# Forming dt of the state space part early, and eleven rotating tiles instead of four for its masked decays, in a hybrid two-layer backbone

## The chip, the cores and the metric

The kernel runs on one core of a Trainium2 chip. The metric is the device time of one execution in microseconds (us); the median of three runs before the change is 1880.62 us (1880.29 to 1880.88). The engines of the core work side by side, each through its own instructions in a fixed order: TensorE (PE in the profile; PEld is its loading of weights), VectorE (DVE), ScalarE (ACT), GpSimd (Pool, written POOL in rows) and SyncE (SP, which issues most DMAs).

## The reference, cut to what matters

Two trunk layers act on 256 context and 256 latent tokens of width 1024. Each layer is a gated feed-forward part, a token mixer and a second feed-forward part. The mixer projects the tokens, splits the width into three groups of heads (a gated linear recurrence, a neighbourhood attention, and a state space part with 8 heads in both directions) and projects the three back. The state space part, in one direction:

```python
    z, xs, bm, cm, dtf, dtb = mamba2_prepare(lat[8], lat[9], lat[10], lat[11], conv_w, conv_b, dt_bias)
    # dtf = softplus(dt_f + dt_bias[0]); xs, bm, cm = silu(conv(...)) split in three
    cum = jnp.cumsum(dtr * A.reshape(G, R), axis=2)
    seg = cum[:, :, :, None] - cum[:, :, None, :]
    Lm = jnp.where(causal[None, None, :, :, None, None], jnp.exp(jnp.minimum(seg, 0.0)), 0.0)
    cb = jnp.einsum('bctgn,bcsgn->bctsg', Cr, Br)
    y_diag = jnp.einsum('bctsg,bctsgr,bcsgr,bcsgrp->bctgrp', cb, Lm, dtr, xr)
    decay_end = jnp.exp(jnp.minimum(cum[:, :, -1:] - cum, 0.0))
    states = jnp.einsum('bcsgn,bcsgr,bcsgrp->bcgrpn', Br, decay_end * dtr, xr)
...
    return rms_norm(y * jax.nn.silu(z), w)
```

The last line is the gate by `z` that closes the state space part.

## The kernel before

All activations stay on the chip; weights stream in from memory. Each large product is made of three products of split halves (lines 675, 676 and 677), here called dense products. They make up most of what PE does. What lies between them, the mixer's small products, is called short here.

The mixer of a layer is written as a table, MIX_ORDER: `feat`, `feats` and `tok` make projections of columns, `go` starts one of the three head groups (`hg` the recurrence, `na` the attention, `ssm` the state space part) as a generator, and `run` advances the started groups. The table gives the program's order. A scheduler then places the instructions of each engine by their priority, which follows the program's order, and by what each waits for; dense products fill the gaps of the groups. Tiles come from rings: a tag of the table TAGS has so many buffers, and a new tile of a tag waits until the tile that had its buffer is no longer read.

The function `dt` has two halves. Lines 1258 to 1280 form dt (its columns come with those of the attention's values, the step `("tok", C_VA)`) and split the decay's exponent into `ah` and `al`. Lines 1285 to 1293 sum it up over tokens on PE, take the exponential on ACT (`ex`, L1288) and form the weights of the states on DVE (L1293).

The function `ssm` then runs in three stages. First, Pool multiplies the inputs by the skip gain (L1307), and six units of the recurrence over chunks follow: weights times inputs into `s` on DVE (L1313), the states on PE (L1317), their copy on ACT (L1321), and the product with C on PE (L1330) with DVE behind it (L1333, L1335). Second, the part inside the chunks: for every chunk of 128 tokens (four in layer 0, two in layer 1) L1342 forms C times B on PE and L1346 masks it on DVE, then for each of the two groups Pool builds four masked decays `gm` with affine_select (L1354), PE sums them (L1358), ACT takes the exponential (L1362) and scales (L1366), DVE combines (L1367, L1369), and PE multiplies with the inputs (L1374); DVE adds the result up (L1376). There are 32 masks in layer 0 and 16 in layer 1. Third, after the projection of `z`: the gate (L1382), squares (L1383), a Newton chain of small DVE operations for the root (L557 to L565), the norm (L1386) and transposes (L1391).

The gate itself, silu of `z`, is formed in `z_in` (L1400), and its tiles `zs` are taken from the ring `gm` too, four in layer 0 and two in layer 1. Next to all this run the attention's scores (L1191), softmax (L1194 to L1205), products (L1207, L1210) and final norm (L1215, a Newton chain, L1218, the transposes L1223). L873 and L874 split the results into `qk` and `mx`, which the output projection reads. L291 and L294 split the incoming weights into halves on ACT and DVE.

Silu and Exp sit in different tables of ACT. When an instruction needs the table that isn't loaded, an ACT_TABLE_LOAD stands ahead of it, under the same line.

Of the kernel before, what the change touches and what calls it, by code (L numbers as in the profile page):

```python
# [38 lines left out]
NORM_PRIO = 200  # L39
NGW = 10  # L40
TAGS = {"V": 1, "V2": 1, "ga": 1, "T": 1, "kS": 1, "gs": 2, "h2": 6, "mx": 4, "qk": 4, "n2": 4, "cv": 1, "bc": 4, "xf": 2,
        "bt": 1, "gm": 4, "ew": 2, "cb": 1, "s2": 3}
FPARTS = [range(0, NF // 2), range(NF // 2, NF)]


C_Q, C_FF, C_FB, C_I, C_G = 0, 256, 512, 768, 1024
C_QA, C_KA, C_VA = 1280, 1536, 1792
C_Z, C_XBC, C_DT = 2048, 2560, 3584
C_XS, C_B, C_C = C_XBC, C_XBC + 512, C_XBC + 768
# [108 lines left out]
def second(n):  # L158
# [13 lines left out]
MIX_ORDER = [  # L172
    [
        ("feats", C_FF, C_FB, C_Q, C_G), ("go", "hg", 0), ("feat", C_QA + 128), ("tok", C_I),
        ("feat", C_XS + 384), ("tok", C_VA), ("feat", C_B), ("feat", C_B + 128), ("feat", C_C + 128),
        ("feat", C_C), ("run", 2), ("run", 4), ("feat", C_XS), ("feat", C_XS + 128), ("feat", C_XS + 256),
        ("feat", C_KA), ("dt",), ("go", "ssm"), ("run", 999), ("feat", C_QA), ("feat", C_KA + 128),
        ("go", "na"), ("run", 999), ("feats1", C_FF + 128, C_FB + 128, C_Q + 128, C_G + 128), ("go", "hg", 1),
        ("run", 999), ("tok", C_Z), ("tok", C_Z + 256), ("run", 999),
    ],  # L180
    [
        ("feats", C_FF, C_FB, C_Q, C_G), ("go", "hg", 0), ("tok", C_I), ("run", 999), ("tok", C_VA),
        ("feat", C_B), ("feat", C_KA), ("run", 6), ("feat", C_C + 128), ("run", 999), ("feat", C_QA),
        ("feat", C_B + 128), ("feat", C_C), ("feats1", C_FF + 128, C_FB + 128, C_Q + 128, C_G + 128),
        ("go", "hg", 1), ("run", 999), ("feat", C_XS), ("feat", C_XS + 128), ("feat", C_XS + 256),
        ("feat", C_XS + 384), ("dt",), ("go", "ssm"), ("run", 999), ("feat", C_KA + 128),
        ("feat", C_QA + 128), ("go", "na"), ("run", 999), ("tok", C_Z), ("tok", C_Z + 256), ("run", 999),
    ],
]
# [1372 lines left out]
```

## Time and profile before

| | us |
|---|---|
| median of three runs | 1880.62 |
| profiled execution | 1881.97 |
| its span on the core | 1880.2 |
| PE busy | 1852.1 |
| DVE busy | 1317.0 |
| ACT busy | 724.8 |
| Pool busy | 59.3 |

The profiled execution is one more run, taken with the profiler; its span is the time from its first to its last instruction. A row of a timeline gives the start, the length, the engine, the line of the kernel, the operation, output and input, and in brackets how long the engine was idle before it and which instruction ended that. A product's row is longer than its share of PE's time, since products overlap: the starts of neighbouring rows tell the pace. The mixer of layer 0 lies between about 445 and 690 us of the span, that of layer 1 between about 1470 and 1690.

### The profile page before, as it was taken

What the parts mean: (1) busy time and instruction counts of PE and PEld (TensorE: products, weight loads), DVE (VectorE), ACT (ScalarE), POOL (GpSimd) and SP (SyncE); (2) the same over time, 40 slices, a digit from 0 to 9 for tenths busy, and PEclk for the clock granted to TensorE, in tenths of its full rate; (3) what the DMA queues carried; (4) which work ended last, traced back from release to release, by engine and by line L of the source; (5) the groups of instructions that cost most, each with busy time, mean ns of one, the idle gap of its engine ahead of it and who ended that gap; (6) DMA issues with size and microseconds to landing.
All of it is one profiled execution on the core that took longest, in us unless ns stands there. A gap on an engine that the chain in (4) does not pass through costs nothing.

```text
span 1880.2 us, 28238 instructions
## 1 busy us (share of the span) xinstructions
PE 1852.1 (99%) x11235; PEld 1596.1 (85%) x11235; DVE 1317.0 (70%) x2324; ACT 724.8 (39%) x1160; POOL 59.3 (3%) x76
## 2 busy tenths in 40 slices
PE   9999999999999999999999999999999999999998
PEld 7788888899777889888888898888889987889998
DVE  7677877875877677677733557777637668887565
ACT  4332223334425544232223342222234455465454
POOL 1000000000014000000000000000000000210000
PEclk9999999999999999999999999999999999999999
DMA  8466666634212134566533536666434422245554
GB/s 307 156 193 194 197 190 194 185 138 124 79 40 62 47 116 143 163 195 192 163 94 101 158 112 189 193 194 194 126 101 154 144 91 74 91 142 183 181 180 134
DMA packets 76964, 277.83 MB, mean 148 GB/s; under 512 B 8608, under 2 KB 10016, under 8 KB 76320
## 3 DMA queue, kind: packets, MB, share of 16 engines
q1 hardware_dynamic: 75312, 272.88, 46.2%
q10 hardware_dynamic: 1520, 3.15, 0.5%
q8 instruction: 88, 1.44, 0.3%
q14 instruction: 44, 0.36, 0.1%
HBM read 269.71 MB, written 5.24 MB: 146 GB/s over the span
## 4 chain that ended last, share of the span: by engine, by line
PE 92%; DVE 6%; ACT 1%; issue 1%; DMA 0%; SPq 0%; DVEq 0%; ACTq 0%
PE psd L675 28%; PE psd L676 27%; PE psd L677 27%; PE psm L1069 1%; DVE junk L516 1%; PE psm L1191 1%; PE psm L1207 1%; PE psm L1317 1%; PE psm L1374 1%; DVE ew L1367 1%; PE psm L1330 1%; DVE lo L294 0%; PE psm L1358 0%; PE psm L592 0%; PE psm L578 0%
## 5 line engine op out<-in xcount | busy, mean ns | idle before, releaser
L294 DVE TENSOR_TENSOR lo<-raw,hi 128x1024 fp32r<-128x1024 f32 x328 | 403.7, 1231 | 369.0 <-ACT hi L291 365.4
L291 ACT CAST hi<-raw 128x1024 fp32r<-128x1024 f32 x332 | 348.6, 1050 | 715.8 <-PE psd L676 664.5
L675 PE MATMUL psd<-h,hi 128*128 128x512 f32 (+1 forms) x1456 | 539.0, 372 | 2.0 <-ACT h L655 1.0
L676 PE MATMUL psd<-h,hi 128*128 128x512 f32 (+1 forms) x1456 | 537.7, 370 | 0.5 <-DVE h L656 0.5
L677 PE MATMUL psd<-h,lo 128*128 128x512 f32 (+1 forms) x1456 | 536.5, 370 | 0.2 <-DVE lo L294 0.2
L516 DVE CUSTOM_DVE_ANT_0 junk<-wm,csb,par 128x1024 bf16<-128x1024 f32 x256 | 327.8, 1280 | 2.4
L675 PEld LDWEIGHTS psd<-h,hi 128*128 128x128 f32 x1456 | 273.5, 189 | 50.0 <-issue 1.5
L677 PEld LDWEIGHTS psd<-h,lo 128*128 128x128 f32 x1456 | 274.1, 188 | 48.4 <-issue 1.5
L676 PEld LDWEIGHTS psd<-h,hi 128*128 128x128 f32 x1456 | 274.6, 189 | 45.6 <-DVE h L656 0.9
L675 PE MATMUL psd<-gh,hi 128*128 128x512 f32 (+1 forms) x605 | 216.8, 358 | 0.0
L677 PE MATMUL psd<-gh,lo 128*128 128x512 f32 (+1 forms) x605 | 216.4, 358 | 0.0
L676 PE MATMUL psd<-gl,hi 128*128 128x512 f32 (+1 forms) x605 | 216.4, 358 | 0.0
L675 PEld LDWEIGHTS psd<-gh,hi 128*128 128x128 f32 x605 | 114.3, 189 | 17.0 <-ACT gh L813 0.3
L676 PEld LDWEIGHTS psd<-gl,hi 128*128 128x128 f32 x605 | 114.2, 189 | 16.7
L677 PEld LDWEIGHTS psd<-gh,lo 128*128 128x128 f32 x605 | 114.2, 189 | 16.7
L676 PE MATMUL psd<-raw,hi 128*128 128x258 f32 x352 | 99.7, 284 | 0.0
L675 PE MATMUL psd<-raw,hi 128*128 128x258 f32 x352 | 99.6, 284 | 0.0
L677 PE MATMUL psd<-raw,lo 128*128 128x258 f32 x352 | 99.3, 284 | 0.0
L813 ACT CAST gh<-silu 128x512 fp32r<-128x512 f32 (+1 forms) x88 | 49.7, 566 | 86.0 <-DVE silu L810 83.6
L544 DVE SCALAR_TENSOR_TENSOR x<-psd,gate,x 128x256 f32<-128x256 f32 x112 | 52.0, 480 | 36.6 <-PE psd L677 35.8
L675 PE MATMUL psd<-hi,h 128*128 128x256 f32 (+1 forms) x224 | 65.9, 295 | 1.4 <-ACT ga L1037 1.3
L675 PEld LDWEIGHTS psd<-raw,hi 128*128 128x128 f32 x352 | 67.0, 190 | 0.0
(276 smaller groups left out, 2435.5 us busy)
## 6 DMA issues: line engine op xcount, KB each, us to landing
raw<-in_wst SPq DMA_DIRECT2D x349, 512.0 KB, 3.6
wm<-in_wmod SPq DMA_DIRECT2D x128, 512.0 KB, 4.1
ws<-in_wm SPq DMA_DIRECT2D x8, 512.0 KB, 9.9
xd<-x SPq DMA_DIRECT2D x2, 2048.0 KB, 6.5
x<-xd SPq DMA_DIRECT2D x8, 512.0 KB, 4.1
wc<-in_wmod SPq DMA_DIRECT2D x7, 512.0 KB, 10.0
x<-in_xt SPq DMA_DIRECT2D x4, 512.0 KB, 5.3
n<-in_bias SPq DMA_DIRECT2D x8, 256.0 KB, 3.3
```

Of the source, the lines that this page charges most:

```text
L291: cut = nc.scalar.copy(hi, r)
L294: ins = e.tensor_tensor(out=lo, in0=r, in1=hi.bitcast(F32), op=ALU.subtract)
L516: self.nc.vector.tensor_tensor_reduce(junk, w, self.csb[:, v], 1.0, self.p(l, "bmod", j), ALU.mult, ALU.add, accum_out=self.mod[l][:, j, v ...
L544: ins = nc.vector.scalar_tensor_tensor(out=self.x[:, d, a:b], in0=ps[:, a - off:b - off], scalar=gate[:, d, v:v + 1], in1=self.x[:, d, a:b ...
L675: mm(ps, wh, xh, start=start, stop=False)
L676: mm(ps, wh, xl, start=False, stop=False)
L677: mm(ps, wl, xh, start=False, stop=stop)
L813: nc.scalar.copy(a[:, lo:hi], s[:, lo:hi])
L1069: nc.tensor.matmul(ps[r, s], kc[r, s], q(r, c * 64), start=True, stop=True)
L1191: nc.tensor.matmul(ps[:, :nk], self.qk[h2][r, t * P:(t + 1) * P], self.qk[2 + h2][r, :nk], start=True, stop=True)
L1207: nc.tensor.matmul(ps[:, hc], pT[:, k * P:(k + 1) * P], self.V[:, k, 256 + h * 64:256 + h * 64 + 64], start=k == 0, stop=k == nk // P - 1)
L1317: nc.tensor.matmul(ps[:, g * 256:g * 256 + 256], bt[:, t, g * P:(g + 1) * P], xw[:, g * 256:g * 256 + 256], start=True, stop=True)
```

## The change

Three edits. The step `("dt",)` stands directly behind `("tok", C_VA)` in both layers, and no longer in front of `("go", "ssm")`. The ring `gm` has 11 buffers of 2 KB per partition instead of 4. The memory for them comes from the scratch space that the program keeps for DMAs with descriptors made at run time, which is set to 1024 bytes.

```diff
 TAGS = {"V": 1, "V2": 1, "ga": 1, "T": 1, "kS": 1, "gs": 2, "h2": 6, "mx": 4, "qk": 4, "n2": 4, "cv": 1, "bc": 4, "xf": 2,
-        "bt": 1, "gm": 4, "ew": 2, "cb": 1, "s2": 3}
+        "bt": 1, "gm": 11, "ew": 2, "cb": 1, "s2": 3}
...
-        ("feat", C_XS + 384), ("tok", C_VA), ("feat", C_B), ("feat", C_B + 128), ("feat", C_C + 128),
+        ("feat", C_XS + 384), ("tok", C_VA), ("dt",), ("feat", C_B), ("feat", C_B + 128), ("feat", C_C + 128),
         ("feat", C_C), ("run", 2), ("run", 4), ("feat", C_XS), ("feat", C_XS + 128), ("feat", C_XS + 256),
-        ("feat", C_KA), ("dt",), ("go", "ssm"), ("run", 999), ("feat", C_QA), ("feat", C_KA + 128),
+        ("feat", C_KA), ("go", "ssm"), ("run", 999), ("feat", C_QA), ("feat", C_KA + 128),
...
-        ("feats", C_FF, C_FB, C_Q, C_G), ("go", "hg", 0), ("tok", C_I), ("run", 999), ("tok", C_VA),
+        ("feats", C_FF, C_FB, C_Q, C_G), ("go", "hg", 0), ("tok", C_I), ("run", 999), ("tok", C_VA), ("dt",),
...
-        ("feat", C_XS + 384), ("dt",), ("go", "ssm"), ("run", 999), ("feat", C_KA + 128),
+        ("feat", C_XS + 384), ("go", "ssm"), ("run", 999), ("feat", C_KA + 128),
...
-    nc = bacc.Bacc("TRN2", target_bir_lowering=False, num_devices=1)
+    nc = bacc.Bacc("TRN2", target_bir_lowering=False, num_devices=1, dynamic_dma_scratch_size=1024)
```

The order of instructions moves at three places. The first is DVE in layer 0, ahead of the first state of the state space part. The names are those of the program, with the numbers of tiles left in; `ga`, `T` and `dec` belong to the recurrence. Before:

```order
L1094 TENSOR_TENSOR ga_3568<-ga_3568,T_3569 128x16x32 x2
L1096 TENSOR_TENSOR T_3569<-T_3569 128x2x8
L1100 COPY dec_4455<-T_3569 128x16
L1293 TENSOR_TENSOR dtk_3898<-ex_4411,dtk_3898 128x4x8 x2
L1313 TENSOR_TENSOR s_712_4442<-x,dtk_3898 128x512
```

and with the change:

```order
L1094 TENSOR_TENSOR ga_3568<-ga_3568,T_3569 128x16x32 x2
L1313 TENSOR_TENSOR s_712_4442<-x,dtk_3898 128x512
L1096 TENSOR_TENSOR T_3569<-T_3569 128x2x8
L1100 COPY dec_4455<-T_3569 128x16
L1333 TENSOR_TENSOR s_716_4452<-psm_4449,ex_3936 128x512
```

L1293 now stands some 48 rows further up, between convolutions, and L1313 comes directly behind L1094. On PE the five products of L1285 leave the place ahead of L1105 in the same way and stand some 180 rows further up.

The second is ACT at the end of layer 1's mixer. `ew` and `cb` belong to the state space part, `n` to the attention, `hi` to the weights' split, and `gm` here are the tiles `zs`. Before:

```order
L1366 ACTIVATE ew_13876<-cb_13860,dtk_12898 128x128
L1366 ACTIVATE ew_13906<-cb_13860,dtk_12898 128x128 x4
L1205 COPY n_2225_14146<-psm_14141 128x512
L1215 ACTIVATE n_2226_14153,nss_13989<-no_13990 128x256
L291 CAST hi_14437<-raw_14435 128x1024
L1362 ACTIVATE ew_13906<-psm_13893 128x512
L1400 ACT_TABLE_LOAD
L1400 ACTIVATE gm_14247<-psd_14186 128x256
L1400 ACTIVATE gm_14248<-psd_14186 128x256
L1215 ACTIVATE n_2227_14155,nss_13989<-no_13991 128x256
```

and with the change:

```order
L1400 ACT_TABLE_LOAD
L1400 ACTIVATE gm_14248<-psd_14186 128x256
L1400 ACTIVATE gm_14247<-psd_14251 128x256
L1366 ACTIVATE ew_13876<-cb_13860,dtk_12898 128x128 x2
L1362 ACT_TABLE_LOAD
L1362 ACTIVATE ew_13876<-psm_13863 128x512
L1366 ACTIVATE ew_13876<-cb_13860,dtk_12898 128x128 x2
L1366 ACTIVATE ew_13906<-cb_13860,dtk_12898 128x128 x4
L1205 COPY n_2225_14146<-psm_14141 128x512
L1215 ACTIVATE n_2226_14153,nss_13989<-no_13990 128x256
L1400 ACT_TABLE_LOAD
L1400 ACTIVATE gm_14248<-psd_14251 128x256
```

Behind the last of these rows stand another load and L1362 for `ew_13906`, and ahead of the first a load, one L1400, a load and L1362 for the unit before. So the four L1400 have moved from behind the last L1362 to places between the L1362, and where one load stood there are six.

The third is PE at the same place, from the last but one L1374 on. L1358 reads the masks, L1207 belongs to the attention, and `mx` and `qk` in a dense product name what the output projection reads. Before:

```order
L1374 MATMUL psm_13887<-x,ew_13876 128x64 x4
L1358 MATMUL psm_13893<-gm_13894,slr 128x512
...
L1207 MATMUL psm_14134<-V_12552,n_2225_14146 128x64 x4
L1374 MATMUL psm_13917<-x,ew_13906 128x64 x4
L675 MATMUL psd_14401<-mx_12776,hi_14284 128x256
...
L677 MATMUL psd_14402<-mx_13502,lo_14285 128x256
L1223 MATMUL psm_14172<-con,no_13990 128x128
L1223 MATMUL psm_14179<-con,no_13990 128x128
```

and with the change:

```order
L1374 MATMUL psm_13887<-x,ew_13876 128x64 x4
L1358 MATMUL psm_13893<-gm_13894,slr 128x512
...
L1207 MATMUL psm_14134<-V_12552,n_2225_14146 128x64 x4
L675 MATMUL psd_14402<-mx_12776,hi_14284 128x256
...
L677 MATMUL psd_14402<-mx_13535,lo_14285 128x256
L1374 MATMUL psm_13917<-x,ew_13906 128x64 x4
L1223 MATMUL psm_14172<-con,no_13990 128x128
L1223 MATMUL psm_14172<-con,no_13991 128x128
```

Where 24 dense products stood between the last L1374 and L1223 there is none; 12 stand ahead of that L1374, and 12 of another bank ahead of the third one. Further up, nine and twenty dense products stood between L1342 and the first L1374, where there are now four and four, and the 21 others stand ahead of L1342. Behind the first L1374 are now 24 dense products, up to the second, where three were.

On Pool the first eleven masks of a layer now stand in one row ahead of L1307, where four did.

## Rows read from the trace of the kernel before

**Rows 1.** The page, parts 1 and 4: busy time of each engine, and the chain.

```profile
PE 1852.1 (99%) x11235; PEld 1596.1 (85%) x11235; DVE 1317.0 (70%) x2324; ACT 724.8 (39%) x1160; POOL 59.3 (3%) x76
...
PE 92%; DVE 6%; ACT 1%; issue 1%; DMA 0%; SPq 0%; DVEq 0%; ACTq 0%
```

**Rows 2.** PE's waits: line <- what it waited for: us in all, times, longest.

```profile
PE psm L1374 <- DVE ew L1369: 3.8, 6, 0.8
PE psm L1317 <- DVE s L1313: 2.4, 3, 2.0
...
PE psm L1223 <- DVE no L1218: 1.0, 1, 1.0
```

**Rows 3.** Pool's idle time ahead of L1354: until which instruction, us, times.

```profile
  PE psm L1358: 91.2, 10
```

**Rows 4.** Timeline of Pool, layer 0: start, length, instruction [idle before <-releaser].

```profile
471.06 0.64 POOL L1354 TENSOR_SCALAR_AFFINE_SELECT gm<-ah 128x512 fp32r<-128x512 f32 x1 [420.49 <-ACT ah L1279]
```

**Rows 5.** Timeline of PE, layer 0, first unit of the state space part.

```profile
525.38 1.13 PE L1317 MATMUL psm<-s,bt 128*128 128x256 f32 x4 [2.02 <-DVE s L1313]
...
527.19 1.96 PE L1330 MATMUL psm<-s,bc 128*128 128x256 f32 x4 [0.18 <-ACT s L1321]
```

**Rows 6.** Timeline of DVE at the same place.

```profile
521.78 0.90 DVE L1096 TENSOR_TENSOR T<-T 128x16 f32<-128x16 f32 x1
...
523.59 1.13 DVE L1293 TENSOR_TENSOR dtk<-ex,dtk 128x32 f32<-128x32 f32 x2
524.64 0.68 DVE L1313 TENSOR_TENSOR s<-x,dtk 128x512 f32<-128x512 f32 x1
```

**Rows 7.** Stretches: length, busy PE, PEld, DVE, ACT, POOL, granted clock, DMA.

```profile
528.00:529.00 1.00, 1.00 (x3) 0.34 (x2) 0.00 (x0) 0.00 (x0) 0.00 (x0) 0.50 0.00 0
1630.70:1657.00 26.30, 22.68 (x161) 19.95 (x159) 23.70 (x61) 18.35 (x43) 9.96 (x12) 1.00 0.26 81
```

**Rows 8.** Timeline of PE, end of the mixer of layer 1.

```profile
1629.74 1.13 PE L1330 MATMUL psm<-s,bc 128*128 128x256 f32 x4
1630.71 0.61 PE L1342 MATMUL psm<-bc,bc 128*128 128x128 f32 x4
...
1633.51 0.36 PE L676 MATMUL psd<-lo,h 128*128 128x256 f32 x1
1633.71 0.28 PE L677 MATMUL psd<-hi,h 128*128 128x256 f32 x1
1633.83 0.28 PE L675 MATMUL psd<-hi,h 128*128 128x256 f32 x1
...
1637.60 1.08 PE L1374 MATMUL psm<-x,ew 128*128 128x64 f32 x8 [0.65 <-DVE ew L1369]
...
1648.16 1.08 PE L1374 MATMUL psm<-x,ew 128*128 128x64 f32 x8 [0.81 <-DVE ew L1369]
...
1651.73 1.08 PE L1374 MATMUL psm<-x,ew 128*128 128x64 f32 x8 [0.67 <-DVE ew L1369]
...
1656.97 0.70 PE L1223 MATMUL psm<-con,no 128*128 128x128 f32 x4 [0.98 <-DVE no L1218]
...
1658.13 0.74 PE L675 MATMUL psd<-qk,hi 128*128 128x256 f32 x4 [0.45 <-ACT qk L873]
```

**Rows 9.** Timeline of ACT at the same place.

```profile
1650.26 0.60 ACT L1362 ACTIVATE ew<-psm 128x512 f32<-128x512 f32 x1 [1.10 <-PE psm L1358]
1650.87 1.28 ACT L1400 ACT_TABLE_LOAD   x1
1652.17 0.66 ACT L1400 ACTIVATE gm<-psd 128x256 f32<-128x256 f32 x2
```

**Rows 10.** Timeline of DVE at the same place.

```profile
1634.34 2.52 DVE L1367 SCALAR_TENSOR_TENSOR ew<-cb,dtk,ew 128x128 f32<-128x128 f32 x5
1636.78 0.68 DVE L1369 TENSOR_TENSOR ew<-ew 128x512 f32<-128x512 f32 x1
...
1649.61 1.22 DVE L294 TENSOR_TENSOR lo<-raw,hi 128x1024 fp32r<-128x1024 f32 x1
```

## The prediction

> **What bounds the kernel now.** Read the page first: TensorE (PE) is busy 1852.1 of 1880.2 us and holds 92% of the chain that ended last [rows 1]. So the kernel ends when PE has done its products, and an edit counts only by the time that PE waits. Next read the list of PE's waits: L1374 (the second product of the state space part, on `ew`) 3.8 us in six waits, L1317 (its state product, on `s`) 2.4, L1223 (the transpose of the attention output) 1.0 [rows 2]. No wait for `gm` is in that list: it is Pool that waits for PE, 91.2 us in ten waits, to get a `gm` tile back [rows 3]. A longer ring by itself takes no wait from PE; it acts through the order in which the scheduler then places the work, and through L1400, whose `zs` tiles come out of the same ring.
>
> **Part one: dt early.** Up to L1280 the chain of dt on DVE and ACT runs early already: Pool's first mask of layer 0 uses its result at 471.06 us [rows 4], fifty microseconds before the state space part starts. What moves are L1285 (PE), L1288 (ACT) and L1293 (DVE). In layer 0 these three are what PE waits for now: DVE runs L1096, L1100, L1293 and L1313 one after the other up to 525.32 [rows 6], and L1317 starts at 525.38 after 2.02 us of waiting [rows 5]. [...] Counting the wait (2.02), the small wait behind it (0.18), 0.83 on L1330 and some 0.5 on the neighbours in the half-speed stretch, 3.5 us go here. In the changed order L1313 stands in front of L1096, so it starts at about 521.8 and, stretched as its neighbours are by Pool's L1307, ends at about 522.8, when PE comes out of its transposes. What is late next is L1330, behind the copy of `s` on ACT, about 0.5 us with nothing but short products beside it. Term: -3.0 (from -1.5, if the clock falls all the same, to -3.5). The moved L1285 costs PE the same where it now stands, and the moved L1293 runs between convolutions; the table load of L1288 goes away in layer 0. In layer 1 nothing waits for dt, and its early place buys nothing.
>
> **Part two: eleven tiles.** Pool issues eleven masks at once and PE's order changes round them. In layer 0 the L1374 waits are 3.8 less the three of layer 1 (0.65, 0.81, 0.67 in [rows 8]), so 1.7; the attention steps now fall two units later and with them more is placed between, and I take half, -0.9 (0 to -1.7). Each return from short to dense products costs about 0.08: behind L1203 the second and third dense products start 0.20 apart, the next pair 0.12 [rows 8]. PE changes from dense to short seven times less in layer 0, four in layer 1: -0.6 and -0.3. Against that, the attention of layer 0 ends later, so L1223 and what hangs on it come where less dense work is left. That is the place which in layer 1 costs 0.98 and 0.45 [rows 8]; I take +1.4 (0 to +2.5). Layer 0 together: -3.0 - 0.9 - 0.6 + 1.4 = **-3.1**.
>
> The end of layer 1's mixer is where the change costs. Count from the start of L1342 (1630.71), and walk the new rows of PE, ACT and DVE with the durations of before; when PE is ready follows from the products that stand ahead in its new row, at the pace that the same products have now.
> First L1374: DVE runs five L1367 of 0.50 from 2.1 on and then L1369, 0.6 [rows 10], so it can start at 5.2. PE is there at 3.4, since 21 dense products (0.12 each, 2.5 us) that stood here are done earlier. Wait 1.8.
> Second: 24 dense products stand ahead of it and cover the first pair of table loads. No wait.
> Third: ACT now alternates. L1400 needs the Silu table and L1362 the Exp table, and each change is a load of 1.28 [rows 9]. Where one load stood there are six. Load, Silu, load and 0.60 for L1362 [rows 9] end at 15.3; four L1367 (two of them held until L1366 has run behind it), one more for the next unit and L1369 lead to 17.6. PE is ready at 15.0. Wait 2.6.
> Fourth: load, Silu, load and L1362 again, ending at 21.9, L1369 at 22.5; PE ready at 21.1. Wait 1.4.
> L1223: before, 24 dense products lie between the last L1374 and L1223; now none. DVE has L1376, L1382, two casts L294 of 1.22 [rows 10], two interleaved Newton chains of small operations, one of which waits for the last L1383 behind two casts on ACT, and only then L1218. That ends at about 29.0, and PE waits 5.9 where it waited 0.98.
> Before, L1223 starts at 26.26 [rows 8]; now at 29.0, with 2.5 us of its products taken out, which is 2.7 + 2.5 = 5.2 lost. Behind it `qk` waits for seven more Newton steps of DVE, 1.4 instead of 0.45, and L1391 for about 0.5: +1.4. Two small waits of L1317 earlier in this layer (0.4 of the 2.4 [rows 2]) and 0.3 of changes fall away, so +5.9. Last, the clock: after 2.02 us of waiting it fell [rows 5, 7], after the 0.98 at L1223 no such row follows, and 5.9 is far beyond both. Its price is what the fall took in layer 0, 0.83 and 0.5: +1.3. Layer 1 together: **+7.2**, with bounds from +0.5 (if the new waits are filled as those of before were) to +9.
>
> [...] The profile shows a load of 1.28, and L1400 starts 1.30 after the load did [rows 9]. [...]
>
> Costed at nothing: the smaller scratch space of DMA, since every issue on the page is on SP's or ACT's queue and none comes from Pool; the bias loads that pass raw weight loads on SP's queue, since none of PE's waits of any size is for a load [rows 2]; two table loads in the next feed-forward part, ACT being busy 39% [rows 1], at most 0.5 if they meet its start. Eleven masks in a row on Pool, 0.64 each [rows 4], 7 us in all, lie beside the convolutions of DVE at 471 us; four lie there already, and if the other seven hold DVE up, I put it at no more than 0.5.
>
> **Sum.** -3.1 + 7.2 = +4.1. On the profiled execution (1881.97, its span 1880.2) that is 1886.1; it lies 1.35 above the median, so on the median of 1880.62 the forecast is **1884.7 us**.
>
> **Rivals.**
> *The end of layer 1 is filled after all (faster).* Only layer 0's gain counts. For it: of the 26.3 us ACT is busy only 18.35 [rows 7], so loads may lie where it waits. DVE is busy 23.70 of them, which leaves it little room. Against it: no dense row is left between the last L1374 and L1223. It decides if layer 1 ends at its good bound, +0.5, and layer 0 beyond its middle: with all of the L1374 waits and the clock gone and no price at L1223 layer 0 gives -3.5 - 1.7 - 0.6 = -5.8; halfway between that and -3.1 it is -4.5, so -4.0 in all, 1876.6.
> *The change moves only what no one waits for (same).* The chain of dt on DVE was early, the ring never held PE. For it: [rows 3]. Against it: the wait at 525.38. Also here: layer 1 costs about 3 and cancels layer 0's gain. 1880.6, within 2.
> *Slower than the forecast.* Layer 0 keeps the clock's fall (-1.5) and pays the full 2.5 at its L1223, so that with -0.9 and -0.6 it gives -0.5; and the clock falls twice at layer 1's end, after the third L1374 (2.6) and before L1223, 7.2 + 1.3 = 8.5: +8.0, 1888.6. It decides from where a wait of 2.6 brings the clock down.
>
> **How the numbers follow.** Forecast 0.47, filled 0.20, same 0.20, slower still 0.13. About 0.2% (3.8 us) is what a measurement of this kernel can tell from no change. The forecast's own range is 1883 to 1887, and its lower part lies within that bound: 0.13 of its 0.47. So faster 0.20, same 0.13 + 0.20 = 0.33, slower 0.34 + 0.13 = 0.47. The range reaches halfway into the faster rival and into the slowest: 1876.6 to 1888.5, and leaves out some 0.17.
>
> **What would show it.** Right: the 2.02 wait at L1317 in layer 0 is gone and the granted clock stays at 1.00 from 520 to 531; six ACT table loads round L1400 and L1362 in layer 1; L1223 there waits over 4 us and a stretch of 0.50 follows. Wrong: L1374 and L1223 of layer 1 wait as before although the loads are there (then the walk charged waits that ran beside others); or layer 0's wait has only moved to L1330 or L1105 (then term one fails); or PE's time differs outside the two mixers, which nothing here explains.

## The result and the profile after

The changed kernel takes 1902.27 us (median of four runs, 1899.55 to 1907.26) against 1880.45 for the one before: a ratio of 1.0119, with a 95% interval of 1.0100 to 1.0139. It is 21.8 us slower, where 4.1 had been forecast and the upper end of the range stood at 1888.5. The profiled execution takes 1903.57 (span 1901.8).

The page of the changed kernel, parts 1 and 2 (busy time, the granted clock in 40 slices), answering to [rows 1]:

```profile
PE 1864.9 (98%) x11235; PEld 1606.0 (84%) x11235; DVE 1317.9 (69%) x2324; ACT 733.6 (39%) x1166; POOL 55.9 (3%) x76
...
PEclk9999999999999999999999999999999999889999
```

PE has the same 11235 products and is busy 12.8 us longer, though nothing was added to it: much of the loss is time in which the same products ran at a lower clock (over the whole span the granted clock is 0.988 on average, where it was 0.995). The rest is mostly waiting. PE's waits of the changed kernel (line <- what it waited for: us in all, times, longest), answering to [rows 2]:

```profile
PE psm L1223 <- DVE no L1218: 5.8, 2, 4.8
PE psm L1374 <- DVE ew L1369: 3.7, 4, 2.2
PE psm L1159 <- DVE h L1153: 3.6, 1, 3.6
PE psm L1374 <- issue: 2.5, 1, 2.5
PE psm L1203 <- ACT n L1198: 1.7, 1, 1.7
```

L1317, second in [rows 2] with 2.4, has 0.8 left and is not among these. L1223 and L1374 had been foreseen. L1159 and L1203 had not: the first is a product with the root of a norm inside the linear recurrence, the second the transpose of the softmax numerators.

Where the time goes is read by setting the starts of the same PE instruction in two traces beside each other: what the distance between two such instructions has grown by is what the stretch has lost. The stretches are named by their place in the kernel before; the kernels other than the changed one are those of the next section. The last column is worked out from the granted clock of each trace: how many us TensorE spent at 0.50 in the three places, in the order of the columns. The kernel before spent 3, 0 and 0 there in its profiled execution.

| lost against the kernel before, us | to 456 | mixer of layer 0, 456 to 695 | layer 1, 1494 to 1535 | end of layer 1's mixer, 1588 to 1680 | all | at 0.50 in the three places, us |
|---|---|---|---|---|---|---|
| forecast | 0 | -3.1 | 0 (at most 0.5) | +7.2 | +4.1 | 0, 0, one fall |
| changed kernel | -2.3 | +4.6 | +6.9 | +12.4 | +21.6 | 7, 7, 20 |
| the same, another execution | -1.1 | +4.6 | +5.6 | +6.9 | +16.0 | 7, 3, 7 |
| dt_only | +1.8 | +2.5 | +1.6 | +0.5 | +6.0 | 0, 0, 0 |
| l0_only | -1.6 | +5.6 | 0 | -0.1 | +3.5 | 7, 0, 0 |
| tiles_only | -2.3 | -2.4 | +5.5 | +7.9 | +8.8 | 0, 7, 14 |
| gm8 | +1.0 | +5.2 | +3.1 | +7.5 | +16.8 | 7, 0, 7 |
| held | +2.3 | +4.5 | +6.9 | +4.8 | +18.1 | 7, 7, 10 |
| held_pin | -0.6 | +5.1 | +1.0 | +5.1 | +10.6 | 7, 0, 10 |
| nosilu | -2.0 | -0.8 | +7.0 | +6.9 | +10.9 | 0, 7, 14 |
| scratch_only | -2.0 | -1.6 | 0 | +4.2 | +0.7 | 0, 0, 10 |
| l0_zs | -0.9 | +16.5 | 0 | 0 | +15.2 | 27, 0, 0 |
| zs_only | +0.2 | +10.7 | 0 | 0 | +10.9 | 20, 0, 0 |

All other stretches together stay within 0.4 in every row. The first column moves by two microseconds either way (by -2.0 in scratch_only too, whose instructions stand in the order of before), and nothing that the change moves lies in it. Three places are left, and none has the size that was forecast.

What the lower clock costs is read where one order of instructions was profiled more than once. scratch_only has the order and the waits of the kernel before; 10 us at 0.50 at the end of layer 1 cost it 4.2, and the 3 us at 0.50 that the kernel before had behind L1317, and scratch_only hadn't, are worth 1.4. The two executions of the changed kernel differ by 14 us at 0.50 and by 5.4 us (12.37 and 6.93) at the end of layer 1. So each microsecond at 0.50 costs some 0.4, an estimate from these three pairs. Taken off, 1494 to 1535 costs the changed kernel an estimated 4.2 in both executions, and the end of layer 1 also 4.2 in both.

A second thing makes the rows easier to read. The kernels dt_only, held and held_pin have their instructions in the same order on every engine but Pool, and the changed kernel and gm8 share PE's order with them up to about 1645 us. In the stretches before that, these five differ by Pool's masks and by the clock alone: the eleven tiles by themselves move nothing else there, once dt is early.

**Layer 1, 1520 to 1536.** Pool's eleven masks now stand in a row, and at the same time DVE has a Newton chain for which L1159 waits. Timelines of the changed kernel: Pool, then DVE, then PE.

```profile
1523.18 0.64 POOL L1354 TENSOR_SCALAR_AFFINE_SELECT gm<-ah 128x512 fp32r<-128x512 f32 x1
1523.77 0.63 POOL L1354 TENSOR_SCALAR_AFFINE_SELECT gm<-al 128x512 fp32r<-128x512 f32 x1
1524.35 0.64 POOL L1354 TENSOR_SCALAR_AFFINE_SELECT gm<-ah 128x512 fp32r<-128x512 f32 x1
```

```profile
1523.28 0.54 DVE L563 TENSOR_TENSOR nw<-nw 128x4 f32<-128x4 f32 x1
1523.86 0.55 DVE L564 SCALAR_TENSOR_TENSOR nw<-nw 128x4 f32<-128x4 f32 x1
1524.45 0.55 DVE L565 SCALAR_TENSOR_TENSOR nw<-nw 128x4 f32<-128x4 f32 x1
...
1527.38 0.16 DVE L563 TENSOR_TENSOR nw<-nw 128x4 f32<-128x4 f32 x1
```

```profile
1528.42 0.41 PE L1159 MATMUL psm<-con,h 128*128 128x128 f32 x2 [3.59 <-DVE h L1153]
```

An operation on four columns takes 0.55 while masks run and 0.16 once they have ended. Each starts 0.1 behind the start of a mask, and the next one 0.58 later, which is the pace of the masks: one operation of the chain gets through for each mask. The wait at L1159 is 3.59 now; in the kernel before it was

```profile
1524.84 0.41 PE L1159 MATMUL psm<-con,h 128*128 128x128 f32 x2 [1.34 <-DVE h L1153]
```

Behind it the clock falls (last rows of this section). That a chain stretches so stood in the trace of before too, beside the four masks there (L563 at 1520.54 takes 0.54, at 1521.90 0.16); the prediction did not look at that stretch.

**Layer 0, 630 to 645.** Timelines of ACT, then PE:

```profile
630.81 1.28 ACT L1400 ACT_TABLE_LOAD   x1 [0.91 <-PE psd L677]
632.10 0.38 ACT L1400 ACTIVATE gm<-psd 128x256 f32<-128x256 f32 x1
632.50 1.28 ACT L1198 ACT_TABLE_LOAD   x1
633.80 0.47 ACT L1198 ACTIVATE n<-psm,nsm 128x256 f32<-128x256 f32 x1
```

```profile
634.42 0.44 PE L1203 MATMUL psm<-con,n 128*128 128x128 f32 x2 [1.70 <-ACT n L1198]
```

The attention now runs later than the gate in layer 0, so the Silu of `z` falls between two Exps of the softmax: load, Silu, load, Exp, and PE waits for the Exp. dt_only has the same wait, tiles_only hasn't: it comes with the early dt.

**End of layer 1.** PE, answering to [rows 8]:

```profile
1641.51 0.61 PE L1342 MATMUL psm<-bc,bc 128*128 128x128 f32 x4
...
1647.05 1.08 PE L1374 MATMUL psm<-x,ew 128*128 128x64 f32 x8 [2.48 <-issue]
...
1665.19 1.62 PE L1374 MATMUL psm<-x,ew 128*128 128x64 f32 x8 [2.24 <-DVE ew L1369]
...
1676.77 1.16 PE L1223 MATMUL psm<-con,no 128*128 128x128 f32 x4 [4.77 <-DVE no L1218]
```

The waits stand where the prediction's walk put them, but for the fourth L1374, which waits for nothing in this execution. The first names no releaser; L1369 on DVE ends at 1646.95, so it is the same wait as the other. Then the clock, in stretches of the changed kernel (length, busy PE, PEld, DVE, ACT, POOL, granted clock, DMA), answering to [rows 7]:

```profile
520.00:531.00 11.00, 9.32 (x93) 6.85 (x92) 9.17 (x20) 2.34 (x4) 4.43 (x4) 1.00 0.10 40
634.00:642.00 8.00, 7.51 (x50) 5.42 (x51) 2.61 (x8) 4.40 (x9) 0.00 (x0) 0.57 0.01 2
1528.00:1536.00 8.00, 6.34 (x24) 5.43 (x25) 4.96 (x9) 3.43 (x5) 0.00 (x0) 0.57 0.35 96
1648.00:1660.00 12.00, 12.00 (x54) 10.10 (x52) 4.62 (x8) 5.45 (x9) 0.63 (x1) 0.57 0.16 46
1665.00:1670.00 5.00, 4.81 (x24) 4.45 (x25) 1.53 (x7) 4.36 (x7) 0.00 (x0) 0.66 0.00 0
1675.00:1684.00 9.00, 7.09 (x37) 6.61 (x38) 6.09 (x26) 2.84 (x8) 0.03 (x1) 0.62 0.36 125
```

Behind or within each of the new waits of layer 0's L1203 and of layer 1 begins a stretch that is for the most part at 0.50 (635 to 641 us in layer 0): once in layer 0, four times in layer 1.

### The profile page after: what moved, and what is told of

It is laid out like the page before. It is cut to its first block, busy times and chain, and to the rows that moved or that the text cites. A ratio compares the mean times of both kernels' runs of the same rounds, so it can differ in the third digit from the quotient of the medians.

```text
span 1901.8 us, 28245 instructions
## 1 busy us (share of the span) xinstructions
PE 1864.9 (98%) x11235; PEld 1606.0 (84%) x11235; DVE 1317.9 (69%) x2324; ACT 733.6 (39%) x1166; POOL 55.9 (3%) x76
## 3 DMA queue, kind: packets, MB, share of 16 engines
q10 hardware_dynamic: 1520, 3.15, 0.6%
## 4 chain that ended last, share of the span: by engine, by line
PE 93%; DVE 5%; ACT 1%; issue 1%; DVEq 0%; ACTq 0%
PE psd L675 28%; PE psd L676 27%; PE psd L677 27%; PE psm L1069 1%; PE psm L1191 1%; PE psm L1207 1%; DVE junk L516 1%; PE psm L1374 1%; PE psm L1317 1%; PE psm L1358 1%; DVE lo L294 1%; PE psm L1330 0%; PE psm L592 0%; PE psm L1203 0%; PE psm L451 0%
## 5 line engine op out<-in xcount | busy, mean ns | idle before, releaser
L675 PE MATMUL psd<-h,hi 128*128 128x512 f32 (+1 forms) x1456 | 539.3, 372 | 2.9 <-ACT qk L1169 1.2
L675 PEld LDWEIGHTS psd<-h,hi 128*128 128x128 f32 x1456 | 274.2, 189 | 51.1 <-ACT qk L1169 1.5
L675 PE MATMUL psd<-gh,hi 128*128 128x512 f32 (+1 forms) x605 | 216.8, 358 | 0.0
L675 PEld LDWEIGHTS psd<-gh,hi 128*128 128x128 f32 x605 | 114.3, 189 | 16.9 <-ACT gh L813 0.3
L675 PE MATMUL psd<-raw,hi 128*128 128x258 f32 x352 | 99.7, 284 | 0.0
L676 PEld LDWEIGHTS psd<-raw,hi 128*128 128x128 f32 x352 | 67.0, 190 | 0.0
L675 PEld LDWEIGHTS psd<-raw,hi 128*128 128x128 f32 x352 | 67.0, 190 | 0.0
```

What stands on the lines that cost most here:

```text
L675: mm(ps, wh, xh, start=start, stop=False)
L676: mm(ps, wh, xl, start=False, stop=False)
```

## The experiments

**Each part alone.** dt_only has the two tables of MIX_ORDER and nothing else of the change, tiles_only the ring and the scratch space:

```diff
-        "bt": 1, "gm": 4, "ew": 2, "cb": 1, "s2": 3}
+        "bt": 1, "gm": 11, "ew": 2, "cb": 1, "s2": 3}
...
-    nc = bacc.Bacc("TRN2", target_bir_lowering=False, num_devices=1)
+    nc = bacc.Bacc("TRN2", target_bir_lowering=False, num_devices=1, dynamic_dma_scratch_size=1024)
```

> dt early in both layers, ring of four, scratch as before. Theory (three separate losses): the alternation of Silu and Exp at layer 1's end (12.4 us in the changed kernel) and the burst of eleven masks beside the recurrence's Newton chain (6.9) both need the long ring, so both are gone; the gain at the first L1317 of layer 0 (about -5 up to 600 us) and the loss behind it in layer 0's attention (+7.9 between 600 and 700 us, with the clock at half for some 7 us) come from the early dt alone and stay: about +3 to +6, 1883 to 1887. Rival (the long ring causes all loss): the gain alone is left, 1874 to 1877.

> Ring of eleven and small scratch, dt where it was. Theory: layer 0 keeps its wait of 2.0 at the first L1317 and has no loss between 600 and 700; in layer 1 the eleven masks stretch the Newton chain ahead of L1159 (wait 3.6, clock at half behind it, +7) and the alternation of six table loads costs +12: about +17 to +20, 1898 to 1901. Rival (early dt causes the loss): no change, 1880.5.

Measured: dt_only 1887.3, ratio 1.0042 (1.0028 to 1.0056); tiles_only 1890.65, 1.0058 (1.0041 to 1.0074). Neither part is a gain. The first came out as my theory had it, or a little above; the second came between the two theories, 7 below mine and 10 above its rival. Together they lose 19 us, near the 21.8 of the whole. By place (the table): layer 0 loses through dt alone (+2.5; with tiles alone it gains 2.4, of which 1.4 is the fall of the clock that only the kernel before had there), the other two mainly through the tiles; of the loss in 1494 to 1535 the early dt has 1.6 by itself.

**Six loads at the end of layer 1, or one.** held is the changed kernel with the `zs` tiles and the last unit's masks of each layer in a ring of their own, which keeps the Silu behind the last L1362 in layer 1, as before:

```diff
-        "bt": 1, "gm": 11, "ew": 2, "cb": 1, "s2": 3}
+        "bt": 1, "gm": 7, "gz": 4, "ew": 2, "cb": 1, "s2": 3}
...
-                        gm = self.tt("gm", [P, 4, P], F32R)
+                        gm = self.tt("gz" if t == self.tts[-1] and g else "gm", [P, 4, P], F32R)
...
-            self.zs = {t: self.tt("gm", [P, 512]) for t in self.tts}
+            self.zs = {t: self.tt("gz", [P, 512]) for t in self.tts}
```

> The change, but the last four masks of a layer and the zs tiles share a ring of four of their own and the other masks have seven (eleven tiles in all), so L1400 again waits for the last L1358. One table load at layer 1's end instead of six. Theory: the 12.4 us at layer 1's end go, the burst's 6.9 and layer 0's share stay: about +9 to +11, 1889 to 1892. Rival (the end's loss is the missing dense products, not the table loads): half of it stays, 1896 or more.

Measured: 1896.74, ratio 1.0093 (1.0078 to 1.0108). The total lies 5 above my range and where the rival put it, but the place doesn't bear the rival out: the end of layer 1 loses 4.8 instead of 12.4, and these 4.8 are the clock's. In 1640 to 1680 us dt_only and held, with the same order on all engines but Pool, read

```profile
1640.00:1680.00 40.00, 34.35 (x258) 31.42 (x257) 32.67 (x85) 25.32 (x60) 10.62 (x16) 1.00 0.35 105
```

```profile
1640.00:1680.00 40.00, 34.61 (x204) 29.24 (x204) 29.51 (x81) 19.89 (x49) 3.22 (x5) 0.87 0.21 66
```

and dt_only, without a fall, loses 0.5 at the end. So with the old order there, the loss that isn't the clock's is gone. But held puts back both things at once, the one load and the 24 dense products ahead of L1223; it doesn't part them. PE's waits of held at the end of layer 1:

```profile
PE psm L1374 <- issue: 2.5, 1, 2.5
PE psm L1374 <- DVE ew L1369: 1.4, 2, 0.7
PE psm L1223 <- DVE no L1218: 1.0, 1, 1.0
```

The waits at the last L1374 and L1223 are back at the 0.67 and 0.98 of [rows 8], the first L1374 is not: dt_only has it too, so it belongs to the early dt, and there it costs next to nothing, since the dense products that left this place are done elsewhere. In 1494 to 1535 nothing has changed, 6.9 as in the changed kernel. That sent me to Pool and DVE there.

**Loads without their reason.** nosilu is the changed kernel with the gate's function exchanged for a copy, so that no load stands at L1400; it leaves the Silu of `z` out of what is computed.

```diff
-            self.nc.scalar.activation(self.zs[t][:, j * 256:j * 256 + 256], ps[t], AF.Silu)
+            self.nc.scalar.activation(self.zs[t][:, j * 256:j * 256 + 256], ps[t], AF.Copy)
```

> The change with a plain copy in place of Silu in L1400, so that the gate by z is left without its nonlinearity: the L1400 stand between the L1362 as in the changed kernel, but no table is loaded for them. Theory (the table loads make the end of layer 1 and the L1203 wait of layer 0 slow): the third and fourth L1374 of layer 1 wait under 1 us, no 1.7 wait at L1203 in layer 0 and fewer stretches at half clock; the burst's 7 us near 1525 stay: about +9 to +12, 1889 to 1892. Rival (the missing dense products ahead of L1223 are the cause, the loads beside it): L1223 waits 4 us or more as it does now and the total stays above 1896.

Measured: 1893.17, ratio 1.0068 (1.0052 to 1.0085), between the two. In layer 0 the loss turns from +4.6 to -0.8: without loads there is no wait at L1203, none at L1223 (1.1 in the changed kernel) and no fall of the clock. From 632 us on the scheduler also placed the instructions otherwise, so what is shown is that the loss needs the loads, not how much of it is the loads and how much the order that goes with them. At the end of layer 1 the waits of nosilu are

```profile
PE psm L1223 <- DVE no L1218: 3.7, 1, 3.7
PE psm L1374 <- issue: 2.5, 1, 2.5
```

so the third L1374, and the fourth in the second execution (below), wait for loads, and the 3.7 at L1223 for none. In held, where 24 dense products lie in front of L1223, it waits 1.0: it is these products that it lacks. The 6.9 that nosilu still loses here hold 14 us at 0.50; without them some 1.4 are left of the changed kernel's 4.2 (estimates at 0.4 for each us), so of what isn't the clock's the loads are the larger part.

**The dose of masks.** gm8 is the changed kernel with eight tiles, so with eight masks in the row instead of eleven:

```diff
-        "bt": 1, "gm": 11, "ew": 2, "cb": 1, "s2": 3}
+        "bt": 1, "gm": 8, "ew": 2, "cb": 1, "s2": 3}
```

> The change with a ring of eight. Theory (each mask that stands beside the Newton chain ahead of L1159 stretches it): eight masks in the burst, so the wait at L1159 of layer 1 lies between the 0.95 of four and the 3.87 of eleven, near 2.5; five table loads at the end instead of six; 1895 to 1899. Rival (the wait at L1159 has another cause than the burst): 3.5 or more, or under 1.

held_pin is held with Pool's L1307 and its masks kept in the program's order, which puts all masks behind L1307 and so away from the Newton chain:

```diff
-            nc.gpsimd.tensor_tensor(out=v3(ys[t]), in0=v3(xt[t]), in1=bc8(self.p(l, "dsk")), op=ALU.mult)
+            self.tc.keep_in_program_order(
+                nc.gpsimd.tensor_tensor(out=v3(ys[t]), in0=v3(xt[t]), in1=bc8(self.p(l, "dsk")), op=ALU.mult))
...
-                        nc.gpsimd.affine_select(
+                        self.tc.keep_in_program_order(nc.gpsimd.affine_select(
```

> The kernel with the separate ring for the last masks and zs, and Pool's masks kept in program order, so that all of them come behind L1307 and none stands beside the Newton chain of the recurrence. Theory (the burst stretches that chain): the small operations of the chain take 0.16 to 0.2 each instead of 0.55, the wait at L1159 falls from 3.9 to under 1.5 and the step from 1494 to 1535 us from 6.9 to under 2; about 1889 to 1892 instead of 1896.7. Rival (the chain is slow for another reason, such as L1293 in it): the wait stays above 3.

Measured: gm8 1898.17, ratio 1.0089 (1.0074 to 1.0104), as expected; held_pin 1893.58, 1.0066 (1.0049 to 1.0082), 1.6 above the range. L1159 in dt_only (four masks), gm8 (eight) and held_pin (none there), one row from each trace:

```profile
1527.49 0.41 PE L1159 MATMUL psm<-con,h 128*128 128x128 f32 x2 [0.67 <-DVE h L1153]
```

```profile
1530.82 0.41 PE L1159 MATMUL psm<-con,h 128*128 128x128 f32 x2 [2.21 <-DVE h L1153]
```

```profile
1527.05 0.41 PE L1159 MATMUL psm<-con,h 128*128 128x128 f32 x2
```

and the chain on DVE in held_pin:

```profile
1524.85 0.16 DVE L563 TENSOR_TENSOR nw<-nw 128x4 f32<-128x4 f32 x1
```

With four, eight and eleven masks the wait is 0.67, 2.21 and 3.59 and the stretch loses 1.6, 3.1 and 6.9 (5.6 in the second execution; an estimated 4.2 in both without the clock's fall); with none beside the chain its operations take 0.16 or 0.17, there is no wait, and 1.0 is left. With dt where it was, and so without L1293 in the chain, the wait is 1.34 with four masks (the kernel before) and 4.15 with eleven (tiles_only). held and held_pin differ in Pool's order alone. Masks beside the chain are the cause of this place. Why held_pin lies above its range is open: its four runs spread over 7 us (1888.81 to 1895.69), and in its profiled execution nothing but falls of the clock parts it from dt_only outside this place.

**Layer 0's dt alone, and the ring's memory alone.** l0_only moves `("dt",)` in the table of layer 0 and nothing else; scratch_only sets the scratch space to 1024 and nothing else.

> dt early in layer 0 only, ring of four, scratch as before. Theory: -5 up to 600 us and +7.9 between 600 and 700, layer 1 as before: about +3, 1882 to 1885, and a stretch of half clock near 635. Rival (the loss between 600 and 700 needs the long ring): 1875 to 1877 with no such stretch.

> The smaller scratch space alone; every engine's order is as before. Every theory: no change, 1879 to 1881.

Measured: l0_only 1885.25, ratio 1.0025 (1.0013 to 1.0037), slightly above its range; scratch_only 1881.2, 0.9998 (0.9986 to 1.0009). The scratch space costs nothing. Early dt in layer 0 alone loses time: in layer 0 it has the loads between the Exps and the waits of dt_only (1.70 at L1203, 1.06 at L1223), and the clock falls.

**Holding the gate back in layer 0.** If the early Silu is the cost, then a `zs` tile that isn't to be had until the attention is through should take it away and leave the gain of dt. l0_zs does that on l0_only, zs_only on the kernel before, with the same edit:

```diff
-            self.zs = {t: self.tt("gm", [P, 512]) for t in self.tts}
+            self.zs = {t: self.tt("gm" if self.last else "n2", [P, 512]) for t in self.tts}
```

> dt early in layer 0 only, ring gm of four, scratch as before, and the zs tiles of layer 0 taken from the attention's ring n2, so that every Silu of layer 0 waits for the last softmax: one table load there where that kernel without the edit has five between L1198 and L1400. Theory (the alternation costs layer 0 its gain): no 1.7 wait at L1203, the step from 543 to 695 us within 1 of nothing instead of +4 to +7, and the whole at 1877 to 1880. Rival (the attention's lag costs it, whatever the tables do): +3 or more in that step, 1882 or more.

> The kernel before with the same edit on zs and nothing else: dt stays late, two loads fewer in layer 0. Theory: the wait of 2.0 at the first L1317 stays; a little under before, 1878 to 1880.5. Rival (the edit itself costs, since Silu now comes late for the gate L1382): 1882 or more.

Measured: l0_zs 1900.68, ratio 1.0105 (1.0091 to 1.0119); zs_only 1891.64, 1.0057 (1.0044 to 1.0070). Both miss by far, and both lie where their rivals had them. In l0_zs the first L1400 (ACT), the waits of PE from 620 to 690 us, and the stretch 640 to 680 read

```profile
666.09 1.28 ACT L1400 ACT_TABLE_LOAD   x1
```

```profile
PE psm L1139 <- DVE kS L1127: 1.8, 1, 1.8
PE psm L1203 <- ACT n L1198: 1.6, 2, 1.3
PE psm L1207 <- ACT n L1205: 1.5, 2, 0.7
```

```profile
640.00:680.00 40.00, 35.10 (x298) 29.08 (x299) 19.12 (x70) 12.93 (x31) 0.00 (x0) 0.67 0.05 19
```

The Silu comes 35 us later than in the changed kernel, as meant, and no load stands between the Exps. But there are new waits on the short steps of the attention, and a third of the clock is gone over 40 us. What brings these waits about no run shows. Nor do these two runs show that the early Silu is the cost: the edit on `zs` alone loses 10.7 in layer 0, early dt alone 5.6, and the two together 16.5, about their sum. Early dt costs as much with the Silu held back, beside an edit that has large waits of its own. That the loads are needed for its loss rests on nosilu. No kernel of this study is faster than the one before.

**The same kernel again.** after_again is the changed kernel unaltered, in another execution, to see how much of its loss is the clock's.

> The changed kernel a second time, for one look at its clock. Theory (the waits are fixed by the order, but whether the clock falls behind a wait differs between executions): the waits at L1159 (3.6), L1203 (1.7), the L1374 of layer 1 (2.5, 2.2) and L1223 (4.8) come again within 0.2, the stretches at half clock differ in place or length, and the steps differ by 1 to 4 us with them. Rival (the falls belong to the order): the same stretches at the same places.

Measured: 1898.01, in one run. The table shows the same loss as before in layer 0 and 5.4 us less at the end of layer 1. There its waits and its stretches are

```profile
PE psm L1223 <- DVE no L1218: 4.8, 1, 4.8
PE psm L1374 <- issue: 2.5, 1, 2.5
PE psm L1374 <- DVE ew L1369: 2.2, 1, 2.2
PE psm L1374 <- DVE nw L557: 0.7, 1, 0.7
```

```profile
1640.00:1660.00 20.00, 15.69 (x108) 13.59 (x106) 14.32 (x32) 15.60 (x32) 3.22 (x5) 1.00 0.12 43
1660.00:1680.00 20.00, 13.97 (x90) 13.03 (x91) 12.91 (x46) 12.28 (x27) 0.55 (x3) 0.83 0.30 94
```

The waits are those of the first execution to a tenth, but for 0.7 at the fourth L1374, which had none there. The clock stays at 1.00 over the first two, where it fell both times in the first execution, and falls only at 1670, within the wait for L1223. The two falls more are 14 us at 0.50 and 5.4 us of time.

## Why the prediction was wrong, point by point

Between the forecast of +4.1 and the +21.6 of the profiled execution lie 17.5 us: 6.9 in 1494 to 1535, 7.7 in layer 0 (+4.6 instead of -3.1) and 5.2 at the end of layer 1, less the 2.3 of the first column.

*The walk of layer 1's end: right in its places and waits, and in its sum partly by luck.* The second execution, with one fall of the clock, beside the forecast:

| from the start of L1342, us | forecast | second execution |
|---|---|---|
| first L1374 starts (wait) | 5.2 (1.8) | 5.5 (2.5) |
| second, wait | none | none |
| third | 17.6 (2.6) | 19.0 (2.2) |
| fourth | 22.5 (1.4) | 24.1 (0.7) |
| L1223 | 29.0 (5.9) | 30.0 (4.8) |
| lost in all | 7.2 | 6.9 |

held and nosilu show its two parts: the loads make the third and fourth wait, the dense products taken out make the one at L1223. But the one fall of the second execution lasted 7 us, an estimated 2.7 and not 1.3, so that the waits and the order took an estimated 4.2 and not 5.9: the two errors cancel.

*The clock at the end of layer 1: a mis-sized term.* I took it to fall once there and to cost 1.3, read from one place, layer 0 of before [rows 5, 7]. That price is right for the fall I read it from, which lasted some 3 us. In the profiled execution the clock fell three times and was at 0.50 for 20 us, an estimated 8.2; with the waits and the order 1.7 cheaper than forecast, that makes the 5.2 us by which the end of layer 1 missed. The rival "slower still" had two falls, at the same low price. The premise was wrong too, that a wait of 2.02 brings the clock down: scratch_only, tiles_only and zs_only have the same 2.02 at L1317, and their clock is at 1.00 from 520 to 531.

*"Eleven masks in a row on Pool ... no more than 0.5": the step that failed outright.* The stretch cost 6.9 and 5.6 in the two executions, an estimated 4.2 of it without the clock's fall behind L1159; the early dt alone, with four masks, has 1.6. That 1.6 I had also put at nothing ("In layer 1 nothing waits for dt"): dt_only has a new wait of 1.35 there, of a dense product (L675) for `qk` of L1169, and what makes the rest no run settles. I set the masks beside the convolutions of layer 0, where DVE does large operations, and never asked what stands beside them in layer 1: a chain of a dozen dependent operations with a product waiting for its end. Yet the prediction itself let Pool's L1307 stretch DVE's operations in layer 0: L1096 takes 0.90 beside it [rows 6], and 0.17 in layer 1 of the kernel before (at 1578.86 us), where Pool is idle. L563 to L565 take 0.55 beside masks and 0.16 without, L560 0.55 beside a mask and 0.17 in held_pin. Why these operations slow down beside Pool's no run here shows.

*Layer 0's loads: a step that was missing.* "The table load of L1288 goes away in layer 0" counted a load saved, and I walked ACT's new row only in layer 1. The mixer of layer 0 has eleven loads before and after: L1288's is gone, but from 630 us on the Silu and the Exps have five (L1198, L1400) instead of three, because the lagging attention puts the Silu between two Exps. The stretch 543 to 695 loses 6.2, with new waits at L1203 (1.70) and L1223 (1.1) and a fall of the clock; in dt_only it loses 4.1, with the same waits and no fall; in nosilu, without loads, it has neither and loses 0.8. The two waits are 2.8 of dt_only's 4.1; what the rest is no run settles.

*The -3.0 for dt: it came by the clock, hardly by the edit.* The 0.83 in its sum is L1330's 1.96 [rows 5] less the 1.13 of its twin in layer 1 [rows 8], and the half-speed stretch is the 0.50 of [rows 7]. L1317 waits 0.50 instead of 2.02, and the clock is at 1.00 from 520 to 531, as forecast. But part of the wait has only moved, to L1105, which the prediction had named as the sign that this term fails, and 0.31 to the second L1317:

```profile
521.23 0.63 PE L1105 MATMUL psm<-con,ga 128*128 128x128 f32 x4 [0.68 <-DVE ga L1094]
...
522.58 1.13 PE L1317 MATMUL psm<-s,bt 128*128 128x256 f32 x4 [0.50 <-DVE s L1313]
```

From 482 to 543 the program gains 3.0. Of that, 1.4 is L1285 and its gap, which moved into the stretch before and cost 1.4 there, as the prediction said of L1285, without taking it off the term. Of the 1.6 that stay, 1.4 is the fall of the clock in the kernel before; scratch_only has the wait unchanged and no fall, and is 1.4 shorter at this place than the kernel before. So the part of the gain that the edit itself makes is some 0.2; the rest was a fall that only one of four executions with that wait had.

*The -0.9 for the L1374 waits of layer 0: wrong.* They were 1.7 and are 1.4 for L1369 and 0.3 for another instruction. *The +1.4 for L1223 of layer 0: right in size, not by its reason.* It waits 1.1 and a product behind it 0.5. But dt_only, with four tiles, has both waits, tiles_only and nosilu have none at L1223: it takes the early dt and the loads, and not the eleven tiles. *The -0.6 for fewer changes from short to dense:* tiles_only gains 1.1 from 543 to 695, but no run shows that this is why. *"Nothing outside the two mixers", and nothing for the scratch space and the bias loads: right.*

*ACT's loads: right.* In the changed kernel a load is 1.28 and the next instruction starts 1.29 after the load's start (630.81 to 632.10). At the end of layer 1 it starts 1.29 or 1.30 after the start of five of the six loads, and 1.52 after the first, where 0.24 is a wait for PE's L1358.

So the mechanism that I wrote about at the end of layer 1 was there, and dt's gain in layer 0 hardly was. Two others were left out, both of the kind that I had looked for in one layer only: layer 0 for Pool beside DVE, layer 1 for the loads on ACT. What stays open is how often the clock falls: the falls make a large part of the 21.6, and two executions don't tell which part of them the change brings.

## What to carry to other kernels

More buffers for an engine that is ahead anyway don't leave the rest as it was: here they let Pool run eleven masks in one burst instead of four, and the burst let through one operation of a chain of small dependent DVE operations per mask, one in 0.58 us instead of 0.20; look up what stands beside the burst at every place where it will occur, not at the first. When work moves in one layer, walk the table loads of ACT in all layers. And don't price a fall of the clock from one place: here falls lasted from 3 us (the kernel before) to an estimated 20 (zs_only, from its clock in 640 to 670 us) and cost an estimated 0.4 for each us (1.4 for 3 us, 4.2 for 10), and the same wait had one behind it in one execution and none in another. Before a loss is put down to an edit, set apart what the clock has in it; a second execution, or a kernel with the same order, shows it.

## What the runs showed of the hardware that was not expected

- Pool's masks (0.64 each) and DVE operations on four columns go in step, 0.55 instead of 0.16 for each; L557, which reads a product's result, takes 0.16 beside a mask as well.
- The clock differs between executions where the waits don't. dt_only and held have the same wait at L1203 in layer 0 (1.71 and 1.70); 640 to 645 us of dt_only and of held:

```profile
640.00:645.00 5.00, 5.00 (x57) 3.98 (x54) 2.45 (x5) 3.33 (x6) 0.00 (x0) 1.00 0.01 3
```

```profile
640.00:645.00 5.00, 5.00 (x32) 3.26 (x33) 0.72 (x2) 2.85 (x5) 0.00 (x0) 0.50 0.00 0
```

- It can fall where no wait is longer than 0.7: scratch_only, with the order and the waits of the kernel before, lost 4.2 at the end of layer 1 in its profiled execution, and in 1635 to 1645 us its clock was

```profile
1635.00:1640.00 5.00, 5.00 (x15) 2.99 (x13) 2.63 (x4) 0.60 (x1) 3.83 (x4) 0.52 0.37 110
1640.00:1645.00 5.00, 5.00 (x23) 5.00 (x24) 2.90 (x8) 1.74 (x5) 0.00 (x0) 0.50 0.00 0
```

What decides whether it falls behind a given wait stays open.
